# Memory values projected and folded head by head; second rows' stores on ScalarE's queue; later token sums

## The chip, the cores and the metric

The kernel runs on one core of one Trainium2 chip. The metric is the device time of one execution in microseconds. The core's engines have instruction queues of their own: TensorE (PE in the profile, with PEld for the loading of weights), VectorE (DVE), ScalarE (ACT), GpSimd (POOL) and SyncE (SP), which issues most of the DMA transfers. Each engine takes its instructions in the order in which they were written to its queue, and waits where an operand is not ready; so the order on a queue is part of the program.

## The reference

One layer over 2048 tokens of width 1024, in float32, with three sub-layers, each of which adds a normalised result to the residual stream:

```python
u = rms_norm(h, g_mix_pre[l]); z = u @ w_in[l]
ya = swa_with_sinks(...)     # sliding-window attention over part of z's columns
yh = hgrn2(...)              # gated linear recurrence in chunks over the others
h = h + rms_norm(concatenate([ya, yh]) @ w_out[l], g_mix_post[l])

u = rms_norm(h, g_x_pre[l]); m = rms_norm(mem, g_mem[l])       # mem: 256 tokens
q = u @ wq; k = m @ wk; v = m @ wv                             # 4 heads of 256
s = einsum('bthd,bmhd->bhtm', q, k) * 256 ** -0.5
h = h + rms_norm(einsum('bhtm,bmhd->bthd', softmax(s), v) @ wo, g_x_post[l])

u = rms_norm(h, g_ffn_pre[l])
h = h + rms_norm((silu(u @ w_gate[l]) * (u @ w_up[l])) @ w_down[l], g_ffn_post[l])
```

## The kernel before

**Splitting.** Every float32 operand of a product is split into a hi half that PE multiplies at full rate (written by ScalarE, L1084) and the lo rest (written by VectorE, L1087, raw minus hi). A product is three matmuls: hi by hi, lo by hi, hi by lo.

**Stages.** First come the input projection, the attention and the hgrn recurrence; then a long phase of large products (`jobs`), which computes w_out ("mixed"), scores, values, hidden and down blocks of two token rows (256 tokens) each. Its products are the lines L1247, L1248 and L1249 of PE. An operand reaches them as tiles named `row`, `raw` or `sraw` (loads, L75), split into T and S.

**The fold.** Since the memory is small, the cross-attention's matrices are folded ahead of the large phase by `fold_cross`, a generator: the memory is normalised; its keys are projected (`wk_x`, 8 blocks of 128 columns), and folded with `wq_x` into `qk_d`; its values are projected (`wv_x`, 8 blocks), and folded head by head with `wo_x` into `vo_d`. So scores and values of the large phase need only one product each. A projected block is 24 matmuls of 128 x 256 (L156, L157, L158: eight k blocks, three matmuls each) into one bank of PSUM, from which ScalarE copies the hi half of `kv` (L324) and VectorE the lo half (L325). A fold of one head is 24 matmuls of 128 x 512 (L368, L369, L370): two row blocks of wo, and for each two 128-token halves of the memory (mt) by two halves of the columns (q). They need four banks, `pss` and `psh` twice. ScalarE copies these out (L376, four copies a head into two tiles `x`) and issues their stores from its own queue (L377). Each weight block of wv or wo is loaded from SyncE (`raw`, 512 KB, three tiles in turn) and split into `whi` and `wlo`, of which three sets rotate.

**What runs beside it.** The last hgrn pairs of the recurrence are advanced in turn with the fold (`mix`); they use the banks g and t (`psg`, `pst`). One pair is: the scores of qq by k (L992), a masked copy (L993), the output (L1021, L1022), its norm, written to `on` by VectorE (L1031), the transposes of `on` (L1039) and its gate (L1041). For each step of the recurrence's generator two of the fold's are taken; when the pairs have ended the fold goes on alone.

**Who sets the order.** The program is written as generators that are advanced in turn, and a scheduler places each instruction in its engine's queue by when it expects it to be ready. `self.folded` and `self.halved` mark the place of the fold's third wo load on SyncE, and of its fourth wo split on ScalarE; the first loads and splits of the large phase are queued from there (`phases`).

**The other two places.** A value block writes the normalised tokens of the second residual, transposes them, and, for the blocks n = 4 and 6, adds them to earlier tokens (`token_sums`, in `value_block`). A down block of the first part (c is 0, f0 = 0, three k blocks) stores its two rows of 128 tokens, `y[0]` and `y[1]`, into `y2_d`; parts that follow add to it. ScalarE or VectorE (L1837, L1833) wrote those rows from PSUM.

Of the kernel before, what the change touches and what calls it, by code (L numbers as in the profile page):

```python
# [18 lines left out]
P = 128  # L19
T = 2048  # L20
D = 1024
M = 256
# [14 lines left out]
def f32(ap):  # L37
    return ap.bitcast(F32)
# [10 lines left out]
class Layer:  # L49
# [79 lines left out]
    def raw_tile(self):  # L129
        self._n += 1  # L130
        return self.wp.tile([P, D], F32, tag="raw", name=f"raw_{self._n}", bufs=3)
# [161 lines left out]
    def fold_cross(self):  # L293

        nc, ph = self.nc, self.xp
        gx = ph.tile([P, KT], F32, name="gx")
        self.load(gx, self.I["g_x_pre"].rearrange("r (k p) -> p (r k)", p=P))
        nc.vector.tensor_scalar_mul(gx, gx, float(M) ** -0.5)
        g = self.gain(self.I["g_mem"])
        mT = [ph.tile([P, KT, M], F32R, name=f"mT{i}") for i in range(2)]  # L300
        raw_tile = self.raw_tile
        turn = itertools.count()

        def split_tiles():

            if next(turn) % 3 < 2:
                return self.split_tiles()
            self._n += 1
            return [ph.tile([P, D], F32R, tag=f"w{x}", name=f"w{x}_{self._n}") for x in ("hi", "lo")]

        def columns(w, c0):
            raw = raw_tile()
            self.load(raw, w[c0 // P].rearrange("p k c -> p (k c)"))
            hi, lo = split_tiles()
            self.split(raw, hi, lo, "A")
            return [x.rearrange("p (k c) -> p k c", k=KT) for x in (hi, lo)]

        def projected(w):
            dst = [ph.tile([P, KT, M], F32R, tag=f"kv{i}", name=f"kv{i}_{self._n}") for i in range(2)]
            for j in range(KT):  # L320
                wh, wl = columns(w, j * P)
                ps = self.bank("sh"[j % 2])[:, :M]
                self.mm3(ps, [((wh[:, k, :], wl[:, k, :]), (mT[0][:, k, :], mT[1][:, k, :])) for k in range(KT)])
                nc.scalar.activation(dst[0][:, j, :], ps, AF.Copy)  # L324
                nc.vector.tensor_tensor(dst[1][:, j, :], ps, f32(dst[0][:, j, :]), ALU.subtract)  # L325
                yield dst

        for t in range(M // P):
            m = raw_tile()
            self.load(m, self.I["mem"][t * P:(t + 1) * P, :])  # L330
            u = self.pre_norm(m, g)
            self.transpose_split(u, lambda q: mT[0][:, 4 * q:4 * q + 4, t * P:(t + 1) * P],
                                 lambda q: mT[1][:, 4 * q:4 * q + 4, t * P:(t + 1) * P])
        for kT in projected(self.I["wk_x"]):
            yield
        for d in range(KT):
            th, tl = columns(self.I["wq_x"], d * P)
            o = self.io_tile("x")
            for q in range(2):
                ps = self.bank("sh"[q])  # L340
                for r in range(2):
                    h = 2 * q + r
                    self.mm3(ps[:, r * M:(r + 1) * M],
                             [((th[:, j, :], tl[:, j, :]), (kT[0][:, j, :], kT[1][:, j, :])) for j in (2 * h, 2 * h + 1)])
                sl = slice(q * 512, (q + 1) * 512)
                nc.scalar.activation(o[:, sl], ps, AF.Copy, scale=gx[:, d:d + 1])
            nc.scalar.dma_start(self.qk_d[d * P:(d + 1) * P, :], o)
            yield
        for vT in projected(self.I["wv_x"]):
            yield  # L350
        for h in range(4):
            banks = [[self.bank(k) for k in "sh"] for _ in range(2)]
            for i in range(2):
                j = 2 * h + i
                raw = raw_tile()
                self.load(raw, self.I["wo_x"][j * P:(j + 1) * P, :])
                if j == 2:
                    self.folded = self.traced(mybir.EngineType.SP)
                wh, wl = split_tiles()
                self.split(raw, wh, wl, "A")  # L360
                if j == 3:
                    self.halved = self.traced(mybir.EngineType.Activation)
                for mt in range(2):
                    ms = slice(mt * P, (mt + 1) * P)
                    ah, al = vT[0][:, j, ms], vT[1][:, j, ms]
                    for q in range(2):
                        sl = slice(q * 512, (q + 1) * 512)
                        nc.tensor.matmul(banks[mt][q], ah, wh[:, sl], start=(i == 0), stop=False)  # L368
                        nc.tensor.matmul(banks[mt][q], ah, wl[:, sl], start=False, stop=False)  # L369
                        nc.tensor.matmul(banks[mt][q], al, wh[:, sl], start=False, stop=(i == 1))  # L370
                if i == 0:
                    yield
            for mt in range(2):
                o = self.io_tile("x")
                for q in range(2):
                    nc.scalar.activation(o[:, q * 512:(q + 1) * 512], banks[mt][q], AF.Copy)  # L376
                nc.scalar.dma_start(self.vo_d[(2 * h + mt) * P:(2 * h + mt + 1) * P, :], o)  # L377
            yield
# [1343 lines left out]
    def value_block(self, n):  # L1722
        nc = self.nc
        y, ss, u, o = {}, [], {}, {}
# [12 lines left out]
        def after():  # L1737
# [25 lines left out]
                yield  # L1763
            if o:
                yield
                for i in range(2):
                    yield from self.token_sums(u[i], o[i], n - 4 + i)

        return self.blocks(self.pt_d, n), out, after, None

    def hidden_blocks(self, b, f):
# [33 lines left out]
    def down_block(self, c, f0, nk, n):  # L1805
        nc = self.nc
# [3 lines left out]
        y, x, ss = {}, {}, []  # L1810
# [46 lines left out]
        def after():  # L1857
            if end:
                return
            s2 = self.small("q_s", 4) if last else None  # L1860
            for i in range(0 if late else 2):
                if not c:
                    self.store(self.y2_d[(n + i) * P:(n + i + 1) * P, :], y[i])
                elif last:
                    self.add(y[i], self.y2_d, n + i)
                else:
                    self.add_to(self.y2_d, n + i, y[i])
                yield
            if last:
                if not late:  # L1870
                    yield
                for i in range(2):
                    self.mean_squares(y[i], i, s2)
                yield
                r = self.rstds(s2)
                for i in range(2):
                    nc.vector.scalar_tensor_tensor(y[i], y[i], r[:, i:i + 1], self.g_post, ALU.mult, ALU.mult)
                    self.add_to(self.out, n + i, y[i])
                    yield
# [32 lines left out]
```

## Time and profile before

| What | Value |
|---|---|
| three runs | 2529.07, 2531.3 and 2536.82 us, median 2531.3 |
| profiled execution, its own time | 2531.37 us |
| its span | 2529.7 us |
| its granted TensorE clock | 0.999 |
| PE busy | 2487.0 us, 98% |
| DVE busy | 1778.6 us, 70% |
| ACT busy | 1216.3 us, 48% |
| POOL busy | 329.5 us, 13% |
| chain of waits that ended last: PE, DVE, DMA | 79%, 8%, 6% |
| DMA over the span | 194 GB/s mean |

The span is the time from the first to the last record of the profiled execution; the 1.67 us beside it lie outside the records. Busy time counts only instructions that do work, and with two engines at work at once both count. A granted clock of 0.999 says that the throttle left TensorE at full speed almost throughout. The fold of the values fills about 700 to 757 us of the span, and the first down stage about 2112 to 2227 us; between two stages the large phase runs over without a break where loads and splits are there in time.

### The profile page before, as it was taken

To read this page: it belongs to the slowest core of one execution; us is meant where nothing else is said; L and a number is where in the kernel's file an instruction comes from. 1 tells how busy PE (TensorE), PEld (TensorE's weight loads), DVE (VectorE), ACT (ScalarE), POOL (GpSimd) and SP (SyncE) were. 2 spreads that over 40 slices of the span, in tenths; PEclk is the share of its full clock that TensorE was granted. 3 is DMA by queue.
4 is the path that set the end of the run, shared out by engine and by line. 5 is a ranking of instruction groups with operands and counts; after the bars stand their busy time and mean duration, and the time that the engine had idled before them with its cause. 6 is when DMAs were issued, how large, how long until landed. Compare 5 with 4: busy or idle time off the path is not lost.

```text
span 2529.7 us, 33635 instructions
## 1 busy us (share of the span) xinstructions
PE 2487.0 (98%) x11798; PEld 2071.3 (82%) x11798; DVE 1778.6 (70%) x2904; ACT 1216.3 (48%) x2506; POOL 329.5 (13%) x452
## 2 busy tenths in 40 slices
PE   9999999999999999999999999999999999999998
PEld 8778888888987778878878888888888888878886
DVE  8897478875657899988866655576666657564766
ACT  5463255644555675656743333353333344443543
POOL 4131232211301111112200000000000000000122
PEclk9999999999999999999999999999999999999999
DMA  6556877895987996858945322254354334565876
GB/s 219 167 173 176 232 221 209 217 291 149 313 315 268 310 317 192 252 180 259 342 148 175 125 83 92 75 195 162 134 197 168 118 139 140 183 175 111 230 170 155
DMA packets 347849, 491.92 MB, mean 194 GB/s; under 512 B 63904, under 2 KB 231840, under 8 KB 347680
## 3 DMA queue, kind: packets, MB, share of 16 engines
q1 hardware_dynamic: 334720, 450.98, 54.7%
q0 software_dynamic: 8352, 26.22, 6.2%
q10 hardware_dynamic: 4608, 12.58, 1.4%
q8 instruction: 92, 1.51, 0.2%
q14 instruction: 77, 0.63, 0.1%
HBM read 309.34 MB, written 180.36 MB: 194 GB/s over the span
## 4 chain that ended last, share of the span: by engine, by line
PE 79%; DVE 8%; DMA 6%; issue 2%; ACT 2%; SPq 1%; POOL 1%; DVEq 0%; ACTq 0%; POOLq 0%
PE psm L1249 22%; PE psm L1247 22%; PE psm L1248 22%; PE psg L157 2%; PE psg L158 2%; PE psg L156 2%; DVE S L1087 1%; DVE T L1087 1%; SPq L75 1%; DMA pair<-in_x_dram 1%; DVE sum L1222 1%; DMA vb<-vb_d 1%; DVE scores L915 0%; ACT junk L1618 0%; DVE wlo L1087 0%
## 5 line engine op out<-in xcount | busy, mean ns | idle before, releaser
L1247 PE MATMUL psm<-T,S 128*128 128x512 f32 x2680 | 1034.6, 391 | 12.8 <-ACT part L1262 6.1
L1248 PE MATMUL psm<-T,S 128*128 128x512 f32 x2680 | 1042.9, 390 | 1.4 <-DVE T L1087 1.3
L1249 PE MATMUL psm<-T,S 128*128 128x512 f32 x2680 | 1030.6, 390 | 4.3 <-DVE S L1087 4.2
L1247 PEld LDWEIGHTS psm<-T,S 128*128 128x128 f32 x2680 | 503.1, 188 | 126.0 <-ACT part L1262 10.5
L1249 PEld LDWEIGHTS psm<-T,S 128*128 128x128 f32 x2680 | 503.3, 188 | 112.5 <-DVE S L1087 7.6
L1248 PEld LDWEIGHTS psm<-T,S 128*128 128x128 f32 x2680 | 503.2, 188 | 107.3 <-DVE T L1087 3.3
L1084 ACT ACTIVATE S<-sum 128x512 fp32r<-128x512 f32 (+1 forms) x370 | 223.2, 617 | 376.9 <-PE psm L1249 266.8
L1087 DVE TENSOR_TENSOR S<-sraw,S 128x512 fp32r<-128x512 f32 (+1 forms) x315 | 212.5, 681 | 229.9 <-ACT S L1084 227.3
L1262 ACT ACTIVATE part<-psm 128x512 f32<-128x512 f32 x285 | 168.5, 597 | 260.8 <-PE psm L1249 243.8
L1087 DVE TENSOR_TENSOR S<-sum,S 128x512 fp32r<-128x512 f32 (+1 forms) x388 | 259.1, 677 | 42.9 <-ACT S L1084 40.2
L1084 ACT ACTIVATE S<-sraw 128x512 fp32r<-128x512 f32 (+1 forms) x300 | 184.2, 617 | 111.7 <-PE psm L1249 109.8
L1651 POOL DMA_DIRECT2D y_d<-row x16 | 14.0, 873 | 1079.9 <-DVE row L1833 1018.6
L1087 DVE TENSOR_TENSOR T<-row,T 128x1024 fp32r<-128x1024 f32 (+1 forms) x112 | 131.3, 1189 | 30.7 <-ACT T L1084 30.4
L156 PE MATMUL psg<-u,whi 128*128 128x512 f32 x320 | 129.2, 404 | 0.0
L157 PE MATMUL psg<-u,whi 128*128 128x512 f32 x320 | 127.9, 400 | 0.0
L158 PE MATMUL psg<-u,wlo 128*128 128x512 f32 x320 | 127.8, 400 | 0.0
L1618 ACT ACTIVATE junk<-row 128x512 f32<-128x512 f32 x160 | 99.6, 624 | 45.9 <-DVE row L1640 20.4
L1084 ACT ACTIVATE T<-row 128x1024 fp32r<-128x1024 f32 (+1 forms) x112 | 112.9, 1027 | 14.0 <-DMA row<-d_s 7.1
L1784 DVE TENSOR_TENSOR row<-psm,part 128x512 f32<-128x512 f32 x66 | 44.1, 689 | 71.3 <-PE psm L1249 71.3
L1087 DVE TENSOR_TENSOR wlo<-raw,whi 128x1024 fp32r<-128x1024 f32 x52 | 63.9, 1231 | 34.0 <-ACT whi L1084 25.6
L1833 DVE TENSOR_TENSOR row<-psm,part 128x512 f32<-128x512 f32 x72 | 49.2, 690 | 48.6 <-PE psm L1249 48.5
L919 ACT ACTIVATE S<-scores,w_mn 128x257 f32<-128x257 f32 (+1 forms) x128 | 63.1, 496 | 42.2 <-DVE w_mn L915 25.8
(344 smaller groups left out, 3386.9 us busy)
## 6 DMA issues: line engine op xcount, KB each, us to landing
sraw<-in_w_gate_dram SPq DMA_DIRECT2D x44, 512.0 KB, 3.6
sraw<-in_w_up_dram SPq DMA_DIRECT2D x44, 512.0 KB, 3.5
hid_d<-row SPq DMA_DIRECT2D x44, 512.0 KB, 2.6
sraw<-hid_d SPq DMA_DIRECT2D x32, 512.0 KB, 4.2
sraw<-in_w_in_dram SPq DMA_DIRECT2D x48, 256.0 KB, 3.9
raw<-in_w_in_dram SPq DMA_DIRECT2D x20, 512.0 KB, 5.8
row<-in_w_down_dram SPq DMA_DIRECT2D x20, 512.0 KB, 7.6
row<-d_s SPq DMA_DIRECT2D x20, 512.0 KB, 9.1
```

The costliest lines, as they stand in the source:

```text
L156: nc.tensor.matmul(ps, ah, bh, start=(i == 0), stop=False)
L157: nc.tensor.matmul(ps, ah, bl, start=False, stop=False)
L158: nc.tensor.matmul(ps, al, bh, start=False, stop=(i == n - 1))
L919: nc.scalar.activation(s[:, r, o:], raw[:, r, o:], AF.Exp, bias=mn[:, i:i + 1], scale=-1.0, accum_out=den[:, i:i + 1])
L1084: self.nc.scalar.activation(hi, raw, AF.Copy)
L1087: self.nc.vector.tensor_tensor(lo, raw, f32(hi), ALU.subtract)
L1247: nc.tensor.matmul(ps, s[:, 0, k, :], t[:, 0, k, :], start=st, stop=False, **kw)
L1248: nc.tensor.matmul(ps, s[:, 0, k, :], t[:, 1, k, :], start=False, stop=False, **kw)
L1249: nc.tensor.matmul(ps, s[:, 1, k, :], t[:, 0, k, :], start=False, stop=sp, **kw)
L1262: nc.scalar.activation(t, ps, AF.Copy)
L1618: self.nc.scalar.activation(junk, a, AF.Square, scale=float(D) ** -0.5, accum_out=to)
L1833: nc.vector.tensor_tensor(d, a, b, ALU.add)
```

## The change

Three edits. First, the values are no longer projected for all heads before the fold: for each head its two column blocks of wv are projected, into banks g and t, and then its two row blocks of wo are folded. `projected` takes the banks as an argument; the keys keep s and h. Second, in the first down part the store of the second row (`y[1]`) is issued from ScalarE's queue, that of the first row from SyncE's as before. Third, a value block whose token sums follow yields once more ahead of them.

```diff
--- before.py
+++ after.py
@@ -315,11 +315,11 @@
             self.split(raw, hi, lo, "A")
             return [x.rearrange("p (k c) -> p k c", k=KT) for x in (hi, lo)]
 
-        def projected(w):
+        def projected(w, kinds):
             dst = [ph.tile([P, KT, M], F32R, tag=f"kv{i}", name=f"kv{i}_{self._n}") for i in range(2)]
             for j in range(KT):
                 wh, wl = columns(w, j * P)
-                ps = self.bank("sh"[j % 2])[:, :M]
+                ps = self.bank(kinds[j % 2])[:, :M]
                 self.mm3(ps, [((wh[:, k, :], wl[:, k, :]), (mT[0][:, k, :], mT[1][:, k, :])) for k in range(KT)])
                 nc.scalar.activation(dst[0][:, j, :], ps, AF.Copy)
                 nc.vector.tensor_tensor(dst[1][:, j, :], ps, f32(dst[0][:, j, :]), ALU.subtract)
@@ -331,7 +331,7 @@
             u = self.pre_norm(m, g)
             self.transpose_split(u, lambda q: mT[0][:, 4 * q:4 * q + 4, t * P:(t + 1) * P],
                                  lambda q: mT[1][:, 4 * q:4 * q + 4, t * P:(t + 1) * P])
-        for kT in projected(self.I["wk_x"]):
+        for kT in projected(self.I["wk_x"], "sh"):
             yield
         for d in range(KT):
             th, tl = columns(self.I["wq_x"], d * P)
@@ -346,9 +346,11 @@
                 nc.scalar.activation(o[:, sl], ps, AF.Copy, scale=gx[:, d:d + 1])
             nc.scalar.dma_start(self.qk_d[d * P:(d + 1) * P, :], o)
             yield
-        for vT in projected(self.I["wv_x"]):
-            yield
+        values = projected(self.I["wv_x"], "gt")
         for h in range(4):
+            for _ in range(2):
+                vT = next(values)
+                yield
             banks = [[self.bank(k) for k in "sh"] for _ in range(2)]
             for i in range(2):
                 j = 2 * h + i
@@ -1763,6 +1765,7 @@
                 yield
             if o:
                 yield
+                yield
                 for i in range(2):
                     yield from self.token_sums(u[i], o[i], n - 4 + i)
 
@@ -1860,7 +1863,7 @@
             s2 = self.small("q_s", 4) if last else None
             for i in range(0 if late else 2):
                 if not c:
-                    self.store(self.y2_d[(n + i) * P:(n + i + 1) * P, :], y[i])
+                    (self.store, nc.scalar.dma_start)[i](self.y2_d[(n + i) * P:(n + i + 1) * P, :], y[i])
                 elif last:
                     self.add(y[i], self.y2_d, n + i)
                 else:
```

The line numbers of the changed kernel are 2 higher from L354 on and 3 higher from L1769 on.

On PE, at the last hgrn pair, the order before (`pss_…` is the bank of the first projected block of wv, `psg` and `pst` are the pair's banks, `on` its normalised output):

```order
L1010 MATMUL psg_940_7274<-vb14_7150,kb14_7149 128x128 x4
L992 MATMUL psg_941_7286<-qq15_7283,k115_7281 128x192 x2
L992 MATMUL pst_942_7291<-qq15_7283,k115_7281 128x192 x2
L156 MATMUL pss_964_7425<-mT0_6294,whi_963_7421 128x256
L157 MATMUL pss_964_7425<-mT1_6295,whi_963_7421 128x256
L158 MATMUL pss_964_7425<-mT0_6294,wlo_963_7422 128x256
```

and with the change, where the projections of wv come only behind the pair:

```order
L1012 MATMUL psg_940_7274<-vb14_7150,kb14_7149 128x128 x4
L994 MATMUL psg_941_7286<-qq15_7283,k115_7281 128x192 x2
L994 MATMUL pst_942_7291<-qq15_7283,k115_7281 128x192 x2
L1041 MATMUL psg_954_7374<-ident_83,on14_7263 128x128 x4
L1023 MATMUL pst_955_7384<-vb14_7150,atz1_2520 128x128
L1024 MATMUL pst_955_7384<-W14_7273,q615_7296 128x128
```

So the transposes of `on` (L1041 there) now stand directly behind the scores, with no projection matmuls between.

On ScalarE, from the second head of the fold to the third, before (`x` are the copies of a head's banks, `kv` the copy of a projected block, `whi` a split of a weight block, `S` a split for the large phase):

```order
L324 ACTIVATE kv0_961_7417<-psh_987_7670 128x256
L376 ACTIVATE x_996_7737<-pss_988_7697 128x512
L376 ACTIVATE x_996_7737<-psh_989_7698 128x512
L377 DMA vo_d_70<-x_996_7737 128x1024
L376 ACTIVATE x_997_7741<-pss_990_7699 128x512
L376 ACTIVATE x_997_7741<-psh_991_7700 128x512
L1084 ACTIVATE whi_1005_7769<-raw_1004_7767 128x1024
```

and with the change:

```order
L378 ACTIVATE x_994_7653<-pss_986_7613 128x512
L378 ACTIVATE x_994_7653<-psh_987_7614 128x512
L378 ACTIVATE x_995_7657<-pss_988_7615 128x512
L378 ACTIVATE x_995_7657<-psh_989_7616 128x512
L379 DMA vo_d_70<-x_994_7653 128x1024
L324 ACTIVATE kv0_961_7417<-psg_998_7667 128x256
L379 DMA vo_d_70<-x_995_7657 128x1024
L1086 ACTIVATE whi_1000_7696<-raw_999_7694 128x1024
L1086 ACTIVATE whi_1007_7733<-raw_1006_7731 128x1024
```

The split `whi_…_7696` is that of a wv block, whose projection PE does next; before, only wo splits were left at that point. All 8 loads of wo followed all 8 of wv on SyncE before; now two of each alternate.

At the end of the first down part, SyncE's order before (`y2_d<-row` is a store of a row, `sraw<-hid_d` and `row<-d_s1` are loads for the next part):

```order
L78 DMA y2_d_73<-row_3149_19733 128x1024
L75 DMA row_3164_19804<-in_w_down_dram 128x2x512
L75 DMA row_3165_19806<-in_w_down_dram 128x2x512
L75 DMA row_3171_19827<-d_s1_6222 128x1024
L75 DMA row_3175_19847<-d_s1_6222 128x1024
L78 DMA y2_d_73<-row_3151_19747 128x1024
L75 DMA sraw_3194_19935<-hid_d_72 128x4x256
L75 DMA row_3179_19868<-d_s1_6222 128x1024
L75 DMA row_3180_19870<-d_s1_6222 128x1024
```

and ScalarE's with the change, where the same store of `row_…_19747` stands as L1866:

```order
L1086 ACTIVATE T_3163_19803<-row_3165_19806 128x1024
L1840 ACTIVATE row_3151_19747<-psm_3138_19672 128x512
L1086 ACTIVATE S_3182_19883<-sraw_3137_19670 128x384
L1086 ACTIVATE T_3170_19826<-row_3171_19827 128x1024
L1866 DMA y2_d_73<-row_3151_19747 128x1024
L1264 ACTIVATE part_3172_19838<-psm_3159_19785 128x512
```

On SyncE that row is gone and all others stand as they stood; on ScalarE the store has come in behind the split of a `d_s1` tile. The later token sums leave the order of every engine as it was.

## The prediction

> **What bounds the kernel now.** I read the page's first part, then the chain of waits, then busy time by stretches over the two places that the change touches.
>
> ```profile
> span 2529.7 us, 33635 instructions
> PE 2487.0 (98%) x11798; PEld 2071.3 (82%) x11798; DVE 1778.6 (70%) x2904; ACT 1216.3 (48%) x2506; POOL 329.5 (13%) x452
> ...
> PE 79%; DVE 8%; DMA 6%; issue 2%; ACT 2%; SPq 1%; POOL 1%; DVEq 0%; ACTq 0%; POOLq 0%
> ...
> 700.50:756.80 56.30, 53.62 (x355) 48.39 (x355) 32.05 (x39) 34.45 (x66) 3.41 (x5) 1.00 0.89 311
> 2112.00:2200.00 88.00, 88.00 (x390) 72.88 (x389) 51.59 (x92) 35.20 (x70) 0.00 (x0) 1.00 0.44 152
> 2200.00:2250.00 50.00, 47.65 (x205) 37.85 (x204) 38.11 (x50) 28.83 (x42) 1.86 (x2) 1.00 0.75 238
> ```
>
> Matmul on PE is the bound: 2487.0 of 2529.7 us, so all idle time of PE together is 42.7 us, and the change removes no matmul. It can only move waits. The last three rows (stretch, its length, busy PE, PEld, DVE, ACT, POOL, then granted clock, DMA share, GB/s) are the end of the fold, the first down stage, and its seam with the next. In the fold PE stands for 56.30 - 53.62 = 2.68 us; in the down stage it never stands; in the seam for 2.35 us. These 5 us are all that the parts could win at their places. Two rows of PE's timeline (start, duration, instruction, in brackets the idle time before it and what ended it) name the fold's:
>
> ```profile
> 743.38 0.50 PE L368 MATMUL pss<-whi,kv 128*128 128x512 f32 x1 [1.04 <-ACT x L376]
> 752.42 0.50 PE L368 MATMUL pss<-whi,kv 128*128 128x512 f32 x1 [1.63 <-ACT whi L1084]
> ```
>
> The first is the second head of wo waiting for banks s and h: the ScalarE copies of the head before were still emptying them. The second waits for the hi half of a wo block that came late. 1.04 + 1.63 = 2.67 us is all of the idle time there.
>
> **Fold: what is removed.** The next fence groups the stretch by line and shape (count, busy time, mean ns), with the timelines of ScalarE and SyncE where the two waits arise and a row on the landing of the weight blocks.
>
> ```profile
> L1084 ACT ACTIVATE whi<-raw 128x1024 fp32r<-128x1024 f32 x14 | 14.7, 1060 | 9.3 <-PE psh L157 3.6 <-PE pss L157 3.5 <-DMA raw<-in_wo_x_dram 2.2
> L1087 DVE TENSOR_TENSOR wlo<-raw,whi 128x1024 fp32r<-128x1024 f32 x15 | 18.3, 1229 | 17.7 <-ACT whi L1084 17.7
> L324 ACT ACTIVATE kv<-pss 128x256 fp32r<-128x256 f32 x4 | 1.5, 371 | 0.2 <-PE pss L158 0.2
> ...
> 743.23 0.59 ACT L376 ACTIVATE x<-psh 128x512 f32<-128x512 f32 x1
> 743.71 0.60 ACT L376 ACTIVATE x<-pss 128x512 f32<-128x512 f32 x1
> 744.19 0.61 ACT L376 ACTIVATE x<-psh 128x512 f32<-128x512 f32 x1
> ...
> 743.79 0.35 SPq L75 DMA_DIRECT2D raw<-in_wo_x_dram  x1
> ...
> DMA to landing us min/median/max: 3.8/6.4/10.2
> ```
>
> The four copies of a head run 0.48 us apart. The projections of the next head, which need neither of these banks now (they use g and t), can lie over them: the 1.04 us can go. The loads of wo move up between those of wv, so that the 1.63 us can go too; the last load was issued at 743.79 and lands after 6.4 us at the median. The work itself keeps its length: matmuls of the same count and width. Its cadence shows here:
>
> ```profile
> 704.80 0.41 PE L156 MATMUL pss<-mT,whi 128*128 128x256 f32 x1
> 705.05 0.28 PE L157 MATMUL pss<-mT,whi 128*128 128x256 f32 x1
> 705.17 0.28 PE L158 MATMUL pss<-mT,wlo 128*128 128x256 f32 x1
> ...
> 756.04 0.39 PE L368 MATMUL psh<-whi,kv 128*128 128x512 f32 x1
> 756.27 0.40 PE L369 MATMUL psh<-wlo,kv 128*128 128x512 f32 x1
> ```
>
> A projection matmul starts every 0.12 us (24 a block: 2.9 us), a fold matmul every 0.23 (24 a head: 5.6 us). So the gross gain is at most **-2.67 us**.
>
> **Fold: what is added.** Four places, found by laying those durations along the new orders.
>
> (a) *The last hgrn pair.* The projections fill PE while VectorE makes the decayed output `on`:
>
> ```profile
> 704.28 0.81 PE L992 MATMUL pst<-qq,k 128*128 128x192 f32 x4
> ...
> 708.50 0.60 PE L1039 MATMUL psg<-ident,on 128*128 128x128 f32 x4
> ...
> 705.14 0.46 DVE L993 COPY_PREDICATED atz<-cmask,pst 128x256 f32<-128x256 int32 x1 [0.20 <-PE pst L992]
> 705.60 0.69 DVE L1031 TENSOR_TENSOR on<-pst,h_rs 128x512 f32<-128x512 f32 x1
> ```
>
> Before, matmuls of wv run from 704.80 to 708.50 and `on` (ended 706.29) is long there. Now the projections want banks g and t, which the pair still holds, and the transposes of `on` stand directly behind the scores: PE is free at 704.80 and gets `on` at 706.29. **+1.5 us**; not below 1.1, if the missing filler lets VectorE reach that row 0.4 us sooner.
>
> (b) *Into the first head.* On ScalarE a whi split (1.06 us) stands ahead of the copy of the last kv half that the fold needs: 0 to 1.06, **+0.5**.
>
> (c) *From the second head to the third* (ScalarE's rows with the change, above). PE closes the head's banks with 4 matmuls of 0.23, then has 7 projection matmuls of 0.12: 1.77 us from the first of the four. The next thing it needs is a whi that stands on ScalarE behind four copies (4 x 0.48), a kv copy (0.37, some of it covered) and its own 1.06 us, about 3.75 us from the same point: 2.0 us of idle time. After three matmuls (0.35 us) PE needs the following whi, 1.06 us later: 0.6 more. **+2.6**; 0, only if PE gets to this place more than 2 us behind ScalarE.
>
> (d) *Into the fourth head.* Only three raw tiles exist; the last wo load goes out when VectorE has split the first of that head's two wv blocks. From there PE has two projections, 2 x 2.9 = 5.7 us. The load lands after 6.4, its whi takes 1.06, and the kv copies (0.37) stand behind that whi on ScalarE: 7.8 us. That is 2.1 us too late; with the quickest landing (3.8) nothing, with 7.4 us 3.1. Since the stalls before it have given the loads time, **+1.6**, between 0 and 3.1.
>
> Sum for the fold: 1.5 + 0.5 + 2.6 + 1.6 - 2.67 = **+3.5 us**, from -2.7 + 1.1 = -1.6 (only (a) is certain by the order) up to 1.5 + 1.06 + 2.6 + 3.1 - 2.67 = +5.6. If (a) too is covered by something that I overlook, -2.7. What follows the fold, the first mixed block, starts on PE right behind it, so the shift goes on to the end.
>
> **Does a stall also cost clock?** The rows say: rarely.
>
> ```profile
> 675.95 0.35 PE L1021 MATMUL pst<-vb,atz 128*128 128x128 f32 x1 [1.97 <-DMA vb<-vb_d]
> 1190.10 0.50 PE L1249 MATMUL psm<-T,S 128*128 128x512 f32 x1 [1.77 <-DVE S L1087]
> ...
> 676.00:681.00 5.00, 5.00 (x40) 1.00 1.04 405
> 1190.00:1195.00 5.00, 4.90 (x19) 0.66 1.05 306
> ```
>
> After the wait of 1.97 us the granted clock stays at 1.00 for the next 5 us, after that of 1.77 us it is 0.66, which costs 0.34 x 5 = 1.7 us. Of the two gaps near 2 us shown one lost clock; I leave it out of the sum and put 1.7 us on the upper end. The Trainium skill ("TensorE: Matmul & The Clock Gate", Part 1: The HAM clock gate) has the array fall to half rate only after an idle window of about 3.4 us; by that rule none of (a) to (d) would cost clock, and the sum would stand. The drop behind 1.77 us disagrees with the rule taken strictly, the other row agrees.
>
> **Second rows' stores.** Eight of sixteen `y2_d` stores of the first down stage leave SyncE's queue for ScalarE's. The one place where SyncE waited long is at the seam:
>
> (The profile shows the tensor's name as y_d.)
>
> ```profile
> L78 SPq DMA_DIRECT2D y_d<-row x16: 320/332/972, 2112.7 to 2219.0; - x16
> ...
> 2195.22 2.02 SPq L75 DMA_DIRECT2D row<-d_s  x2
> 2203.99 0.32 SPq L78 DMA_DIRECT2D y_d<-row  x1
> 2205.24 0.37 SPq L75 DMA_DIRECT2D sraw<-hid_d  x1
> 2205.66 1.04 SPq L75 DMA_DIRECT2D row<-d_s  x2
> ...
> 2204.66 0.55 DVE L1087 TENSOR_TENSOR S<-sraw,S 128x384 fp32r<-128x384 f32 x1
> ...
> 2203.39 0.58 ACT L1837 ACTIVATE row<-psm 128x512 f32<-128x512 f32 x1
> ...
> 2212.36 1.06 ACT L1084 ACTIVATE T<-row 128x1024 fp32r<-128x1024 f32 x1 [3.09 <-DMA row<-d_s]
> 2215.93 0.50 PE L1247 MATMUL psm<-T,S 128*128 128x512 f32 x1 [1.83 <-DVE row L1833]
> ```
>
> SyncE issued nothing from 2197.24 until ScalarE's row copy was done at 2203.97, then the store, then a hidden-value load at 2205.24, and only then the `d_s` loads, for one of which ScalarE waits until 2212.36 (3.09 us). Take the store away, and the hidden-value load still waits for its tile: VectorE's split of 2204.66 ends at 2205.21, 0.03 us before that issue. So nothing behind it comes earlier, and the store's own wait was in the shadow of that one. On ScalarE each store is an issue of 0.33 us (8 x 0.33 = 2.6 us in a stage where ScalarE works 35.20 of 88.00 us and PE never stands); it waits there for a row copy that ScalarE itself made a few instructions earlier, so the splits queued behind it are held by the issue alone. At the seam it goes out behind one more split (ScalarE's rows above), about a microsecond later, and so runs beside the `d_s` loads instead of ahead of them, 512 KB among theirs. Bounds: -1.8, if the seam's wait goes after all; +1.0, if the splits behind a store come late by three issues in a row. The covering row (2204.66) decides: **0**. If that cover were gone the store would be worth at most the 1.2 us from 2203.99 to 2205.24.
>
> The Trainium skill ("DMA: Bandwidth & Descriptors", Issuing engines are not separate DMA queues) says the same transfers interleave on the same engines whoever issues them, and that only the sequencer's time is saved; that time is SyncE's 0.33 us a store here, off the bound, and the sum would be as above.
>
> **Later token sums.** One more turn of the generator before `token_sums` for two blocks moves no instruction on any engine: the orders there are the same row by row. **0**, and no end of the range.
>
> **Sum.** The profiled execution took 2531.37 us, 1.67 around the span of 2529.7; the three runs (2529.07 to 2536.82) have their median at 2531.3, so it stands for them. 2531.4 + 3.5 + 0 + 0 = **2534.9 us**, +0.14%. About 0.3%, 7.6 us, is what a measurement of this kernel can tell from no change.
>
> **The rivals.**
>
> *Rival 1, the gain comes through.* Both waits of the fold go, and the walk is too grim: (a) is covered, (c) and (d) vanish, because the loads of wo come sooner in the order and ScalarE runs ahead. 2531.4 - 2.7 = **2528.7**; with (a) alone 2529.8. For it: ScalarE works only 34.45 of 56.30 us there, and the loads move up. Against it: in (a) no matmul stands in the order between scores and transposes, and in (c) the copies stand ahead of the split. Chance 0.25.
>
> *Rival 2, the fourth head runs dry: slower.* One mechanism, the ring of three raw tiles: interleaved, a late block of wv also holds the wo blocks behind it, so the landing (10.2 us at worst) decides instead of 6.4. From 10.2 - 4.3 (5.7 less 1.06 and 0.37) = 5.9 us idle in (d) instead of 1.6, and a gap that long probably loses the clock once: 2534.9 + 4.3 + 1.7 = **2540.9**. It decides from a landing above some 9 us; DMA is 0.89 busy in this stretch, which speaks for it, the median of 6.4 against. Chance 0.1.
>
> *Rival 3, SyncE freed.* The `d_s` loads issue earlier and the wait of 1.83 us goes: 2534.9 - 1.8 = **2533.1**. Against it stands the row at 2204.66. Chance 0.1.
>
> *Rival 4, no effect.* The scheduler's new order of the fold gives and takes the same: 2531.4. That lies between, and holds 0.05. My forecast has 0.5.
>
> **How the numbers follow.** The forecast's own bounds are 2531.4 - 1.6 to 2531.4 + 5.6, 2529.8 to 2537.0. The range reaches below to Rival 1's 2528.7 and a little of the runs' spread, 2528, and above to the upper end with one loss of clock and the stores' +1.0, 2531.4 + 5.6 + 1.7 + 1.0, rounded up to 2541: 2528 to 2541. Faster by over 0.3% (below 2523.7) needs more than all that PE's idle time at both places holds (2531.4 - 5.0 = 2526.4), so only an effect that I don't see: 0.04. Slower by over 0.3% (above 2538.9) takes Rival 2 and a bit of the forecast's tail: 0.11. Within: 0.85.
>
> **What would show each step.** PE's idle rows between 700 and 765: the waits for `x` L376 and for the last whi gone (removed part right); about 1.5 us ahead of the transposes of `on` (a); 2 to 2.6 us for a whi behind the second head's copies (c); a wait for kv or whi ahead of the fourth head (d), its size telling the landing. The mixed block's first L1247 product then stands near 760.2 instead of 756.74. At the seam, the first hidden-value load still issues when VectorE's split ends. The prediction is wrong if (c) or (d) leave no idle time, if the granted clock falls below 0.9 for 5 us or more behind one of them, or if the span changes by more than the fold's end does.

## The result, and the profile after

The changed kernel is slower by 0.21%: ratio 1.0021 to the kernel before, 95% interval 1.0013 to 1.0028, from 21 runs of the changed kernel and 22 of the kernel before (medians 2537.56 and 2531.72 us). One more run of the changed kernel took 10470.73 us and is left out. By the ratio that is +5.3 us, with 3.3 to 7.1 by the interval. It lies inside the forecast range, on the forecast side; it is above the forecast +3.5, which the interval still holds.

The profiled execution took 2535.95 us, 4.6 more than that of before. Its first part of the page, and then PE's idle rows in the fold (start, duration, instruction, in brackets the idle time and what ended it), which answer to the rows at 743.38 and 752.42 of before:

```profile
span 2534.2 us, 33625 instructions
PE 2490.1 (98%) x11798; PEld 2073.8 (82%) x11798; DVE 1779.4 (70%) x2904; ACT 1215.8 (48%) x2506; POOL 330.2 (13%) x452
```

```profile
702.77 0.81 PE L994 MATMUL pst<-qq,k 128*128 128x192 f32 x4
704.92 0.63 PE L1041 MATMUL psg<-ident,on 128*128 128x128 f32 x4 [1.33 <-DVE on L1033]
714.81 0.51 PE L370 MATMUL pss<-whi,kv 128*128 128x512 f32 x1 [0.38 <-ACT kv L324]
737.69 0.39 PE L156 MATMUL pst<-mT,whi 128*128 128x256 f32 x1 [2.87 <-ACT whi L1086]
738.64 0.50 PE L370 MATMUL pss<-whi,kv 128*128 128x512 f32 x1 [0.45 <-ACT whi L1086]
...
759.74 0.40 PE L1249 MATMUL psm<-T,S 128*128 128x512 f32 x1
```

Both old waits are gone (2.67 us) and four new ones have come, 1.33 + 0.38 + 2.87 + 0.45 = 5.03 us. The first and the last row give the measure that I use for all experiments: **the fold's length**, from the start of the last hgrn scores on PE to the first product of the mixed phase. It is 759.74 - 702.77 = 56.97 us here and 756.74 - 704.28 = 52.46 before: 4.51 us longer. This measure leaves out the 700 us ahead of the fold, in which single profiles differ by nearly 6 us for reasons of their own (with three raw tiles, the last scores start between 702.77 and 708.64).

The measure does not begin at quite the same work in both kernels. Before, the first three projection matmuls of wv stand ahead of the last scores:

```profile
700.55 0.28 PE L156 MATMUL pss<-mT,whi 128*128 128x256 f32 x1
700.67 0.28 PE L157 MATMUL pss<-mT,whi 128*128 128x256 f32 x1
700.79 0.28 PE L158 MATMUL pss<-mT,wlo 128*128 128x256 f32 x1
```

With the change all 192 stand behind them. Three matmuls at 0.12 us are 0.36 us, by which the changed kernel's fold measures longer without any loss.

The waits explain 5.03 - 2.67 = 2.36 of the 4.51 us, and the place of the mark 0.36. Most of the rest is clock. By stretches (length, busy PE, granted clock, DMA share, GB/s):

```profile
735.00:740.00 5.00, 1.86 (x9) 0.98 1.04 417
740.00:745.00 5.00, 5.00 (x27) 0.68 1.03 418
2215.00:2220.00 5.00, 2.71 (x12) 1.00 1.04 370
2220.00:2225.00 5.00, 5.00 (x16) 0.66 1.03 410
```

Behind the 2.87 us wait the clock is 0.68 for 5 us, which costs 0.32 x 5 = 1.6 us; before it was 1.00 throughout the fold. Projection matmuls there start every 0.21 us instead of 0.12 for some 3.4 us. With it 2.36 + 0.36 + 1.6 = 4.3 of 4.5 us are accounted for; the remaining 0.2 us I did not trace to rows. A second drop, behind the seam's wait at 2219.70 (2.29 us now, 1.83 before), took 1.7 us more in this execution; the experiments give no sign that it is the change's.

### The profile page after: what moved, and what is told of

Same layout as the page of the kernel before. It is cut to its first block, busy times and chain, and to the rows that moved or that the text cites. A ratio compares the mean times of both kernels' runs of the same rounds, so it can differ in the third digit from the quotient of the medians.

```text
span 2534.2 us, 33625 instructions
## 1 busy us (share of the span) xinstructions
PE 2490.1 (98%) x11798; PEld 2073.8 (82%) x11798; DVE 1779.4 (70%) x2904; ACT 1215.8 (48%) x2506; POOL 330.2 (13%) x452
## 4 chain that ended last, share of the span: by engine, by line
PE 82%; DVE 6%; DMA 5%; ACT 2%; issue 2%; POOL 1%; SPq 0%; DVEq 0%; ACTq 0%; POOLq 0%
PE psm L1251 22%; PE psm L1249 22%; PE psm L1250 22%; PE psg L158 2%; PE psg L157 2%; PE psg L156 2%; DVE S L1089 1%; DMA sraw<-y_d 1%; DVE T L1089 1%; DVE sum L1224 0%; ACT junk L1620 0%; DMA out_s<-u 0%; DMA sraw<-in_w_in_dram 0%; PE psh L994 0%; PE pss L946 0%
## 5 line engine op out<-in xcount | busy, mean ns | idle before, releaser
L1086 ACT ACTIVATE T<-row 128x1024 fp32r<-128x1024 f32 (+1 forms) x112 | 112.9, 1027 | 10.5 <-DMA row<-d_s 6.0
```

What stands on the lines that cost most here:

```text
L1086: self.nc.scalar.activation(hi, raw, AF.Copy)
```

## The experiments

Each is given by its edit against the changed kernel, or against the kernel before where it says so.

**Which part it is.** First the fold alone: stores and token sums as before.

```diff
-                    (self.store, nc.scalar.dma_start)[i](self.y2_d[...], y[i])
+                    self.store(self.y2_d[...], y[i])
...
             if o:
                 yield
-                yield
```

> The kernel before with the fold edit alone; stores and token sums as before. Theory F (the loss lies in the fold: new waits of 1.33, 0.38, 2.87 and 0.45 us for the 2.67 removed, net +2.4, and a stretch of lower clock behind the 2.87 us wait, 1.6 us): the same ratio as the whole change, 1.0015 to 1.0025, and these waits in the profile. Rival S (a part of the loss, the 1.65 us of clock behind the longer wait at 2219.70, comes from the stores on ScalarE's queue): 1.0005 to 1.0015, and the seam's wait back at 1.8 us.

Measured: 1.0021 (1.0011 to 1.0031), the fold 57.37 us long, with waits of 1.33, 0.38, 3.26 and 0.44 us. Second the rest alone, that is the kernel before with the stores and token sums of the change:

```diff
-                    self.store(self.y2_d[...], y[i])
+                    (self.store, nc.scalar.dma_start)[i](self.y2_d[...], y[i])
...
             if o:
                 yield
+                yield
```

> The change without the fold edit: stores on ScalarE's queue and later token sums alone. Theory F: no change, ratio 0.9995 to 1.0005 (the stores' own place on SyncE was hidden behind a split of VectorE). Rival S: slower by 1 to 2 us, 1.0005 to 1.0010. Rival SyncE-freed: the seam's wait of 1.83 us is gone, 0.9993 or less.

Measured: 1.0005 (0.9994 to 1.0016), the fold 52.91 us. The seam's wait at the end of the first down part was 1.45 us in the first and 1.30 in the second of these profiles, against 1.83 before and 2.29 with the whole change. Over all profiles of this study it lies between 1.45 and 2.07 us in the three kernels that store from SyncE alone, and between 0.53 and 2.92 in the ten others, so it follows neither way of storing. The second ratio stands on the border between theory F and Rival S and does not part them. The first does better: with the stores left as they were it has the whole loss. So the fold edit carries the loss, theory F; by the intervals alone, a share of the stores of up to some 4 us is not excluded.

These runs also repeat the measure. The fold edit was profiled twice, at 56.97 and 57.37 us, and the fold of before twice, at 52.46 and 52.91. What is inside repeats less well: the second profile of the old fold has one wait of 1.59 us, with a clock of 0.67 behind it, where the first has 2.67 us of waits and full clock.

In the changed kernel's trace SyncE at the seam does what the prediction said. These are its rows, with the split of VectorE that holds it:

```profile
2207.99 0.55 DVE L1089 TENSOR_TENSOR S<-sraw,S 128x384 fp32r<-128x384 f32 x1
...
2208.57 0.37 SPq L75 DMA_DIRECT2D sraw<-hid_d  x1
2209.04 1.03 SPq L75 DMA_DIRECT2D row<-d_s  x2
```

The split ends at 2208.54 and the load goes out at 2208.57, 0.03 us later as before, though the second row's store no longer stands ahead of it.

**What the 2.87 us wait is: ScalarE's queue?** My step (c) said that PE waits for a split that stands behind copies on ScalarE. The trace after shows one thing more, five splits S for the large phase ahead of the copies. They belong to the marks that say from where the large phase's first loads and splits are queued; the fold's new order brought these marks forward against the weight blocks. The next kernel moves them back.

```diff
-                if j == 2:
+                if j == 4:
                     self.folded = self.traced(mybir.EngineType.SP)
...
-                if j == 3:
+                if j == 5:
                     self.halved = self.traced(mybir.EngineType.Activation)
```

> The whole change, but the two marks from which the large phase's first loads and splits are queued move from the second head's wo blocks (j = 2 and 3) to the third's (j = 4 and 5), where they stood in time before. On ScalarE the five splits S then stand behind the third head's, and the split of the wv block that PE needs between the second and the third head comes ahead of the copies. Theory Q (the 2.87 us wait is ScalarE's queue: splits that wait for a late load, then copies, ahead of the split that PE needs): that wait shrinks below 0.5 us, its clock loss goes with it, and the kernel gains 3 to 4.5 us on the whole change, ratio to before 1.0000 to 1.0008. Rival L (the weight block itself is late, whatever stands ahead of it): the wait stays above 2 us and the ratio at 1.002.

Measured: 1.0019 (1.0009 to 1.0029), the fold 57.60 us. The wait named in (c) is gone, as theory Q wanted, and nothing is gained, as Q did not want. PE's idle rows of that kernel:

```profile
706.40 0.63 PE L1041 MATMUL psg<-ident,on 128*128 128x128 f32 x4 [1.33 <-DVE on L1033]
...
743.34 0.50 PE L370 MATMUL pss<-whi,kv 128*128 128x512 f32 x1 [1.45 <-ACT whi L1086]
...
748.74 0.39 PE L158 MATMUL psg<-mT,wlo 128*128 128x256 f32 x1 [1.35 <-DVE wlo L1089]
758.62 0.50 PE L370 MATMUL pss<-whi,kv 128*128 128x512 f32 x1 [1.32 <-ACT whi L1086]
```

Three waits of 4.12 us in sum stand where 3.32 stood. The first of them is for the split of a wo block whose load was issued at 731.30, right behind four loads of 512 KB for the large phase; by the row on its tile it took 10.8 us to land. So Q as I had put it was wrong, and a new reading was needed.

**Do the waits add up?** Run together with the last one was a kernel that also gives PE its filler back at (a): the first two projected blocks go to banks s and h.

```diff
-                ps = self.bank(kinds[j % 2])[:, :M]
+                ps = self.bank(kinds[min(j, len(kinds) - 2 + j % 2)])[:, :M]
...
-        values = projected(self.I["wv_x"], "gt")
+        values = projected(self.I["wv_x"], "shgt")
```

> As the run with the moved marks, and the first two projected blocks go to banks s and h again, which are free then, so that they can fill PE while the last hgrn pair waits for VectorE. Theory H (the 1.33 us wait is only the missing filler): that wait goes, and 1.3 us more are gained: 0.9990 to 1.0003 against before. Rival: the filler delays the pair's own chain, and the wait moves to the next transposes: no better than with the marks alone.

Measured: 1.0018 (1.0008 to 1.0027), the fold 57.10 us. The 1.33 us wait and the 0.38 us wait are gone, but theory H's gain did not come: the wait at the third head is 4.10 instead of 1.45 us. The two waits behind it fell to 0.80 and 0.76, so that of 1.71 us taken away at the front 0.33 us are left as a gain in waits. Later I ran the same edit with the marks unmoved:

> The whole change, with the first two projected blocks in banks s and h, marks unmoved. If the waits add up as the prediction took them, the 1.33 us ahead of the transposes of `on` goes and nothing else changes: 55.6 us from the last score to the first mixed product. If the fold is fed at a fixed pace by its weight loads (three raw tiles, landings of 10 us), PE only comes earlier to the next missing block: 56.5 to 57.3 us, and the wait ahead of the third head grows by about as much.

Measured: 1.0014 (1.0004 to 1.0023), the fold 56.65 us, and one row says much of why:

```profile
737.13 0.58 PE L156 MATMUL pst<-mT,whi 128*128 128x256 f32 x1 [3.67 <-ACT whi L1086]
```

1.71 us of waits went at the front, and the wait at the third head grew by 0.8 us, since PE comes earlier to a block that lands late. Most of the other 0.9 us went to the clock: behind this wait it was at half for the whole 5 us from 737.13, against 0.71 in the 5 us behind 737.69 with the change, which takes another microsecond. The fold measures 0.3 us shorter, not 1.3, and even that is the place of the mark, since three projection matmuls stand ahead of the scores again. So the fixed pace by the loads is borne out for about half of what was taken away; for the rest the clock, which differs from one execution to the next, hides what the order gained. My sum had taken the waits as independent.

**The load or the queue.** In the changed kernel two things end at the same place ahead of the third head, ScalarE's queue and the landing of the block. The timelines of SyncE and ScalarE, and the landing of the load at 725.60:

```profile
721.00 2.95 SPq L75 DMA_DIRECT2D sraw<-y_d  x4
725.60 0.35 SPq L75 DMA_DIRECT2D raw<-in_wv_x_dram  x1
...
729.20 1.15 ACT L1086 ACTIVATE S<-sraw 128x512 fp32r<-128x512 f32 x2 [0.73 <-DMA sraw<-y_d]
732.13 1.16 ACT L1086 ACTIVATE S<-sraw 128x512 fp32r<-128x512 f32 x2 [1.77 <-DMA sraw<-y_d]
733.55 0.63 ACT L1086 ACTIVATE S<-sraw 128x512 fp32r<-128x512 f32 x1 [0.27 <-DMA sraw<-y_d]
734.09 0.58 ACT L378 ACTIVATE x<-pss 128x512 f32<-128x512 f32 x1
...
735.99 0.41 ACT L324 ACTIVATE kv<-psg 128x256 fp32r<-128x256 f32 x1
736.58 3.11 ACT L1086 ACTIVATE whi<-raw 128x1024 fp32r<-128x1024 f32 x3 [0.18 <-ACT kv L324]
```

```profile
DMA to landing us min/median/max: 10.5/10.5/10.5
```

ScalarE is free at 736.40, and the wv block lands at 725.60 + 10.5 = 736.1: its load stands behind four of the large phase's `sraw` loads, 2 MB, in a stretch where DMA moves 397 GB/s (725.60 to 736.10). The test moves only ScalarE's mark, so that the five splits leave their place and every load stays:

```diff
-                if j == 3:
+                if j == 5:
                     self.halved = self.traced(mybir.EngineType.Activation)
```

> The whole change, with only ScalarE's mark moved (from j = 3 to j = 5): the five splits S leave the place ahead of the second head's copies, the sraw loads and all weight loads stay where they are. In the changed kernel two things ended at the same time ahead of the third head: ScalarE came free at 736.40, and the wv block, issued at 725.60 behind four sraw loads, landed 10.5 us later at 736.1. Theory Q (ScalarE's queue alone): the wait of 2.87 us falls to about 2.0, by the 0.8 us for which the copies had stood behind the splits. Theory D (the late load alone suffices): it stays at 2.3 or more, and the time from the last score to the first mixed product stays at 56.5 to 57.2 us (56.97 with the change, 52.46 before).

PE's two waiting rows, and ScalarE's split with the copy ahead of it:

```profile
739.67 0.38 PE L156 MATMUL pst<-mT,whi 128*128 128x256 f32 x1 [2.41 <-ACT whi L1086]
740.89 0.80 PE L370 MATMUL pss<-whi,kv 128*128 128x512 f32 x1 [0.72 <-ACT whi L1086]
...
737.70 0.42 ACT L324 ACTIVATE kv<-psg 128x256 fp32r<-128x256 f32 x1
738.56 1.06 ACT L1086 ACTIVATE whi<-raw 128x1024 fp32r<-128x1024 f32 x1 [0.44 <-DMA raw<-in_wv_x_dram]
```

Measured: 1.0015 (1.0005 to 1.0025), the fold 56.62 us. With the five splits out of ScalarE's way the two waits are 3.13 us in sum, against 3.32. ScalarE now stands idle for 0.44 us until the block is there, so it is the late load that sets the end of the wait: theory D. The last row also gives the share of the order that step (c) saw. ScalarE is free of copies at 738.12, 0.44 us before the split starts; had the block been there, 2.41 - 0.44 = 1.97 us of the wait would have stayed. So by these rows either of the two, the load or the copies ahead of the split, is enough for a wait of about 2 us.

**The burst and the ring.** The load is late because it stands behind the four `sraw` loads, and it stands there because its tile, one of three, came free only then: it goes out at 725.60, when VectorE ends a split of a raw tile (from 724.35, 1.22 us). Each can be taken away alone. First the burst: the marks go to the fourth head's wo blocks, behind nearly all weight loads (j = 6 and 7 in the lines shown above).

> The whole change, with the two marks at the fourth head's wo blocks (j = 6 and 7): the large phase's six sraw loads (512 KB each) and its five splits now stand behind nearly all weight loads. With the marks at j = 4 and 5 the waits only moved (1.45, 1.35 and 1.32 us, each behind a wo load that took about 11 us to land behind four of these sraw loads). Theory D (these sraw loads, ahead of weight blocks on the transfer queues, make the weight blocks late wherever they are put): the waits for weights after 735 us shrink below 1 us in sum, ratio to before 1.0000 to 1.0010. Rival B (three raw tiles: a block can be fetched only so early, whatever else is on the queues): waits of 2.5 us or more in sum stay. Rival T (the first mixed block then waits for its own splits): the waits move behind the fold, ratio 1.0015 or more.

Measured: 1.0017 (1.0005 to 1.0028), the fold 53.46 us, 3.5 shorter than with the change. One wait is left behind 735 us:

```profile
758.80 0.50 PE L370 MATMUL pss<-whi,kv 128*128 128x512 f32 x1 [1.61 <-ACT kv L324]
```

It stands where step (d) had forecast one, with its releaser and at its size (1.6), but not for its reason. ScalarE's rows there:

```profile
754.81 1.06 ACT L1086 ACTIVATE whi<-raw 128x1024 fp32r<-128x1024 f32 x1 [1.74 <-DMA raw<-in_wo_x_dram]
755.78 2.70 ACT L1086 ACTIVATE S<-sraw 128x512 fp32r<-128x512 f32 x5
758.38 0.36 ACT L324 ACTIVATE kv<-pst 128x256 fp32r<-128x256 f32 x1
```

PE stands from 757.19. The last whi split was done early enough for the kv copy to follow it at 755.78; the five splits S, which this run's own mark put between them, hold the copy back by 2.6 us. So the waits for late weight blocks are gone from the profile, as D has it, and the one that is left was made by the test.

The timed ratio says less: 1.3 to 7 us more than before, where the fold's length gives 1.0 (0.6 without the place of the mark), and it can't be told from the change's own 1.0021. Rival T, waits that move behind the fold, is not what makes it up in the profile: from the first mixed product to the end it has 1772.0 us, before had 1773.0. What the timed runs saw beyond the fold I cannot say. Second the ring: four raw tiles in place of three, marks as in the change.

```diff
-        raw_tile = self.raw_tile
         turn = itertools.count()
+        ring = itertools.count()
+
+        def raw_tile():
+            if next(ring) % 4 < 3:
+                return self.raw_tile()
+            self._n += 1
+            return ph.tile([P, D], F32, tag="wraw", name=f"wraw_{self._n}")
```

> The whole change with four raw tiles in place of three, so each weight block may be fetched one earlier; marks unchanged. Rival B: the 2.87 us wait ahead of the third head shrinks below 1 us, and with it the clock's loss: 1.0000 to 1.0010 against before. Theory Q as it stands for the unmoved marks (ScalarE's queue, in which splits for late sraw loads and the head's copies stand ahead of the split that PE needs): with the fourth tile the wanted split moves up among those splits, the wait falls to 0 to 1.5 us by what the sraw loads leave. If neither holds it stays near 2.9 us and the ratio near 1.002.

Measured: 1.0000 (0.9989 to 1.0011), the fold 52.19 us: no loss is left to see. Its SyncE rows show how:

```profile
722.86 0.33 SPq L75 DMA_DIRECT2D wraw<-in_wv_x_dram  x1
723.28 2.86 SPq L75 DMA_DIRECT2D sraw<-y_d  x4
727.95 1.48 SPq L75 DMA_DIRECT2D raw<-in_wo_x_dram  x2
```

The wv block now goes out ahead of the `sraw` loads and lands in 5.8 us. The first of the two wo blocks behind them takes 11.0 us as ever, but a fourth tile covers it, and PE does not wait behind 735 us. So in the profiles it takes both, the burst and the short ring, to make the wait; in the timed runs only the fourth tile is shown to undo the loss. Neither run parts the load from ScalarE's queue: with the block there in time its split also stands ahead of the head's copies (732.50 against 736.35 here, 736.98 against 738.80 with the late marks). That the load is enough by itself rests on the run that moves ScalarE's mark alone.

**Is interleaving worth anything then?** All mends at once (banks s and h first, marks at j = 6 and 7, four tiles):

> All mends at once: first two projected blocks in banks s and h, marks at j = 6 and 7, four raw tiles. Theory D with B: no wait over 0.5 us in the fold; 2.7 us less than before, ratio 0.9985 to 1.0000. If the seam to the mixed phase takes the waits over: 1.0005 or more.

And the kernel before with four raw tiles alone, the ring's lines as above:

> The kernel before with four raw tiles alone. If the fold before was limited by how early its last block can be fetched, the 1.63 us wait at 752.42 goes and the 1.04 us wait for the banks stays: ratio 0.9990 to 1.0000. If the landing time decides, no change.

Measured: 0.9997 (0.9986 to 1.0007) with a fold of 50.28 us and one wait of 0.54, and 0.9998 (0.9989 to 1.0007) with 49.49 us. With four tiles the old order has no idle row in the fold at all, both its waits gone (I had expected only that at 752.42 to go, and why the other went I did not trace). Its fold is 3.0 us shorter than before and 0.8 shorter than the best interleaved one; both of these begin behind the same three projection matmuls. Neither kernel can be told from the kernel before by its time, since 3 us are 0.12%. So no version is shown to beat the kernel before; by the profiles, what the fold lacked was the tile, not the order.

**What the wait costs beside itself.** To see whether the low clock comes from PE's idle time, 24 transposes of the identity into a spare bank were put on PE where it waits.

```diff
                 vT = next(values)
+                if h == 2 and not filled:
+                    filled.append(1)
+                    with self.queued(self.traced(mybir.EngineType.PE)):
+                        self.turns("g", 24)
                 yield
```

> The whole change, with 24 transposes of the identity into a spare bank put on PE where it waits 2.87 us; nothing reads their result, so the computation is the same. Theory C (the lower clock behind the wait, 0.68 over 5 us, comes from PE's idle time itself and costs 1.6 us beside the wait): with PE busy the granted clock stays at 1.00 there, and the time from the last score to the first mixed product falls from 56.97 to about 55.4 us. Rival (the clock falls there by load on the chip or by chance): the clock drops all the same. If the transposes take longer than the wait, they add their excess, up to 1 us.

PE's rows, the first of them the fill, and then stretches as above:

```profile
740.52 2.78 PE L484 MATMUL psg<-ident 128*128 128x128 f32 x24
743.90 0.39 PE L156 MATMUL pst<-mT,whi 128*128 128x256 f32 x1 [0.60 <-ACT whi L1091]
...
754.72 0.39 PE L156 MATMUL psg<-mT,whi 128*128 128x256 f32 x1 [1.42 <-ACT whi L1091]
755.98 0.39 PE L158 MATMUL psg<-mT,wlo 128*128 128x256 f32 x1 [0.76 <-DVE wlo L1094]
```

```profile
740.00:745.00 5.00, 3.96 (x33) 1.00 1.03 414
745.00:750.00 5.00, 5.00 (x33) 1.00 1.04 418
750.00:755.00 5.00, 3.58 (x17) 1.00 0.50 202
755.00:760.00 5.00, 4.24 (x25) 0.73 0.82 278
```

At the place it went as theory C has it: the clock stays at 1.00 where it was 0.68. But the fold as a whole is 60.02 us long, 3 longer, and the kernel 1.0042 (1.0025 to 1.0059): the scheduler placed the copies of the third head differently, a wv split came behind two of them, and new waits of 1.42 and 0.76 us arose at 754.72 and 755.98, with a clock of 0.73 behind them. So theory C is borne out where the fill stands, in this one profile, and the shorter fold that I expected of it (about 55.4 us) did not come.

## Why the prediction was right, and where not

The number held; of the steps, not all did. By two of the signs that it named itself the prediction is wrong: (d) left no idle time, and the clock fell to 0.68 for 5 us behind (c). The third sign is there too, since the span grew by 4.5 us and the fold's end moved by 3.0, but it shows little: from the first mixed product to the end the thirteen profiles take between 1768.7 and 1774.5 us. That the sum came near is in part luck, because the 1.6 us of (d), which never came, stood in for 1.6 us of clock, which the sum did not have.

- **What bounds, and what can be won.** Right. Both waits of the fold before went, and nothing else was to be had; Rival 1, in which the gain of 2.7 us comes through, fell.
- **(a), the transposes of `on`: +1.5.** 1.33 measured, same place, same releaser.
- **(b), into the first head: +0.5.** 0.38 measured, for a copy of kv, as said.
- **(c), into the third head: +2.6.** 2.87 + 0.45 = 3.32 measured, at the two matmuls named. The size was near and the reason was half of it: I had read it off ScalarE's order alone (copies ahead of the split) with every block landed in time. For that order the 2.0 us of the walk were right (1.97, from the run that moves only ScalarE's mark). But the block landed 10.5 us after its issue, and with ScalarE's splits moved away the wait stayed at 2.41 + 0.72.
- **(d), into the fourth head: +1.6.** 0 measured. I had let the stalls ahead of it take only 0.5 us from it; (c) is 3 us of stall, and the last wo block took 4.4 us to land, not 6.4. No run showed this wait: the 1.61 us with the late marks have another cause.
- **The sum.** (a) to (d) were added as if independent: 6.2 us of new waits, of which 5.03 came. The runs that mend (a) show the error: the wait at the next late block grows in its place.
- **The clock: 0 in the sum, 1.7 on the upper end.** Beside (d) the mis-sized term. Behind (c) it cost 1.6 us, and all six waits of 2.8 us and more did the like (below). With 1.6 for the clock and 0 for (d) the sum would have been +3.5 again, and with (c) at its measured size +4.2, for a fold that became 4.5 us longer. The rule of the Trainium skill ("TensorE: Matmul & The Clock Gate", Part 1: The HAM clock gate) that stood beside it, half rate after an idle window of about 3.4 us, does not agree with this trace taken strictly: a wait of 2.87 us lost the clock.
- **Stores: 0.** Right as far as the runs can tell (1.0005, 0.9994 to 1.0016, token sums included), with the reason: the hidden-value load still goes out 0.03 us behind VectorE's split. Rival 3 fell with it. **Token sums: 0**; they were run only together with the stores.
- **Rival 2, the ring of three tiles.** Its mechanism was nearer to the truth than my (c): the ring with landings above 9 us decided, beside ScalarE's order. Its place was wrong (the third head, not the fourth) and so its price.
- **The range** held: +5.3 on the predicted base of 2531.4 is 2536.7, the measured median 2537.6, both below 2541. The 0.3% that the prediction took for the least that can be told was too much: with 21 and 22 runs 0.21% stands clear of no change.

## What to carry to other kernels

When an order of work is changed, lay the loads beside it too: which transfers of the next phase are queued between those that the new order needs soonest, and how many tiles stand between issue and use. A wait on a split that stands behind copies may be a late load in disguise; the landing of that one load says so. Waits fed by one ring of tiles are not to be added up, since mending one can make the next longer; in the fold's length an extra tile was worth more (3.0 us) than any order tried here.

## What the runs showed of the hardware

How often a wait of PE costs clock was not what I expected. In the thirteen profiles of this study, the waits of PE between 20 and 2510 us of the span, sorted by length, and how many had a granted clock below 0.95 in the 5 us from their end:

| PE's wait, us | waits | with a lower clock |
|---|---|---|
| 0.8 to 1.2 | 64 | 5 |
| 1.2 to 1.6 | 69 | 5 |
| 1.6 to 2.0 | 34 | 7 |
| 2.0 to 2.8 | 17 | 9 |
| 2.8 and more | 6 | 6 |

Where two waits stand within 5 us of each other, one drop is counted for both. Mostly the mean clock of those 5 us is 0.66, so that each drop costs about 1.7 us, beside the wait and about as much for a short wait as for a long one. (One, behind 3.67 us, was 0.50, 2.5 us.) A wait in the same place loses clock in one profile and not in another: at the seam 2.29 us did with the change, and 2.79 us in a later kernel did not. Part of the spread of single runs, 9 us in the kernel before and 11 in the changed one, may come from this; that was not separated. That the idle time itself brings the drop is tested at one place only, with the 24 transposes.
